# Both output products of a macaron block as seven quarter products for eight, on one Trainium2 core

## The chip, the cores and the metric

The kernel runs on one core of one Trainium2 chip. The metric is device time in microseconds (us), the median of several executions.

## The reference, cut to what matters

The block is two SwiGLU layers around an attention mixer, on x of 1024 tokens by D = 1024, all in float32. FF is 2816, 22 blocks of 128.

```python
def rms_norm(x, g):
    x32 = x.astype(jnp.float32)
    y = x32 * lax.rsqrt(jnp.mean(x32 * x32, axis=-1, keepdims=True) + EPS) * g.astype(jnp.float32)
    return y.astype(x.dtype)

def swiglu(h, w_in, w_out):
    gate, up = jnp.split(h @ w_in, 2, axis=-1)
    return (jax.nn.silu(gate) * up) @ w_out
...
    x = x + mix @ w_mix_out
    x = x + 0.5 * swiglu(rms_norm(x, ffn2_norm), ffn2_w_in, ffn2_w_out)
```

Before the mixer stands the first layer, `x + 0.5 * swiglu(rms_norm(x, ffn1_norm), ffn1_w_in, ffn1_w_out)`. The mixer projects the normed x, runs banded and compressed/selected attention, and projects back; nothing in it is touched but how its first projection begins.

## The kernel before, in words

**Precision.** A float32 product is made of three matmuls on operands that are split into a high and a low part (`mm3`, L248: high by high L249, high by low L250, low by high L251). Splitting a 128x512 tile is a copy to the high part on ScalarE (ACT) or GpSimd (POOL) and a subtraction for the low part on VectorE (DVE): `split` L445 with ACT L453 and DVE L457, or `conv` with POOL L87 and DVE L92.

**Order.** Nothing is ordered by hand. The program adds tasks, each with an engine, a cost, a position, what it depends on and the buffers it takes (`Slots`), to a `Plan` (L121). `Plan.run` picks, engine by engine, the task that can start first (the lowest position among those within 0.08) and emits it, so it sets the order of each engine's in-order queue. There are three plans: the first SwiGLU, the projection of the mixer, and attention with the second SwiGLU. All DMAs are issued from SyncE (SP), also in order.

**Input stage** (`first_stage` L566). h @ w_in is made block by block of FF. Two blocks are plain, twenty are seven products for eight (Strassen-Winograd): the operand of tokens is h in four quarters A11 to A22 and sums S1 to S4 of them, kept split in memory; the weights are quarters B11 to B22, which are the gate and up columns for the two halves of D, with differences T1 to T4 of them, made by `less` (L691, POOL, four a block) from raw tiles `wraw`. Each of the seven products of a block is 12 matmuls of 128x512. From banks P, R and Q come gate and up of the two token halves: `keep` L746 (ACT) copies a bank, `plus` L750 (DVE) adds another to it, silu L762 (ACT), and `times` L754 (POOL) multiplies silu(gate) by up. `put` stores the two results, 128x512 each, to DRAM tiles `gs`.

**Output stage** (`second_stage`). Eleven chunks of two FF blocks. For each block `gs` is loaded as a whole (`graw`, 128x1024, 512 KB), split by ACT L814 and DVE L816, and the two halves of w_out's 128 rows are loaded (`wraw`) and split by `conv`. Then each of 8 token tiles by 2 halves of D gets 6 matmuls in a bank of its own, and DVE adds half of the bank to the residual X (L846, `x<-lg,x`, 176 times). X was reloaded at the stage's start (`load_x`, or from XS in the second layer), since the input stage uses X's place for buffers.

**After the first output stage.** `norm_tile` (L531) norms a finished tile (`nxs`, DVE L537) and flips it by 8 transposes on TensorE (PE, `flip4`, L311) into a bank "a"; `flip_hi` and `flip_lo` make the split operand `xn`. Tiles 0 to 5 are in the first plan, 6 and 7 in the second, whose projection then runs with `xn` as the moving operand. The chunk's eight weight units are `CH3`, four of them split in the first plan.

Banks of PSUM: three "a", three "lg", one "pv", one "mo".

Of the kernel before, what the change touches and what calls it, by code (L numbers as in the profile page):

```python
# [8 lines left out]
F32 = mybir.dt.float32  # L9
# [9 lines left out]
T = 1024  # L19
# [168 lines left out]
def block_kernel(  # L188
# [118 lines left out]
    def flip4(src):  # L307

        p = bank("a", name="ntr")
# [126 lines left out]
    def fetch(src, pos, deps=()):  # L436
# [3 lines left out]
        def emit():  # L440
            b["r"] = ws.place()
            dma(b["r"].rearrange("p (k f) -> p k f", k=4), src)
# [3 lines left out]
    def split(b, dep, src_users, pos, eng):  # L446

        w, us = {}, []

        def high():  # L450
            w["h"], w["l"] = ws.pair()
# [4 lines left out]
        highs.append(add(eng, 0.6 if eng == "A" else 0.66, pos, high, deps=[dep], after=highs[-1:], takes=[(r_spl, us)]))  # L456
        low = add("D", 0.69, pos + 0.5, lambda: DVE.tensor_tensor(w["l"], b["r"], w["h"].bitcast(F32), op=OP.subtract),  # L457
                  deps=highs[-1:])
        src_users.extend([highs[-1], low])
# [60 lines left out]
    def flip_task(src, dst, t, pos, deps, free=()):  # L520

        b, au = {}, []
        p = add("P", 0.45, pos, lambda: b.update(p=flip4(src())), deps=deps, takes=[(r_a, au)])
# [5 lines left out]
    def norm_tile(t, pos, dep):  # L529
# [10 lines left out]
        for a in range(2):  # L540
            p, lo = flip_task(lambda a=a: xb["xs"][:, 512 * a:512 * a + 512], lambda a=a: blocks(xn[t // 4])[a], t, pos, [g])
# [24 lines left out]
    def first_stage(layer, w_in, opn, scaled, units_, pos, weigh, at0, pieces, opened, xa=()):  # L566
# [20 lines left out]
        stored_g = [[None, None] for _ in range(NF)]  # L587
# [11 lines left out]
        def put(n, half, buf, at, dep, us):  # L599
            t = add("S", 0.75, at, lambda: dma(GS[layer][n][:, HALF[half]], buf()), deps=[dep], tail=2.2)  # L600
            stored_g[n][half] = t
            us.append(t)

# [8 lines left out]
        for half in range(2):  # L612
            for n in range(PLAIN):
# [33 lines left out]
                put(n, half, lambda buf=buf: buf["u"], at, d, bu)  # L647
# [31 lines left out]
        av = Views([X[4][:, h] for h in HALF], [S3u(0), S1u(0)])  # L679
        dv = Views([X[5][:, h] for h in HALF], [S3u(1), S1u(1)])  # L680
        bv = Views([X[6][:, HALF[0]]], [S3u(2)])
        sv = Views([X[6][:, HALF[1]]], [S1u(2)])

        def less(a, b, at, deps):
# [1253 lines left out]
```

## Time and profile before

| what | us |
|---|---|
| median of three runs | 2025.47 (2023.34 to 2026.98) |
| the profiled execution | 2022.6 |
| its span | 2020.8 |
| PE busy in it | 1957.5 (97%) |
| DVE, ACT, POOL busy | 1249.0 (62%), 782.3 (39%), 692.2 (34%) |

The profile is one execution, with times in us from its start. A row of a timeline gives an instruction's start, its duration, engine, line and operation, and in brackets how long the engine was idle before it and what ended that. Matmuls overlap, so their spacing and not their duration is what one costs. A window's row gives the busy time of each engine in that stretch with the number of instructions, then the granted clock of PE as a share of the full one.

### The profile page before, as it was taken

How to read it: one execution, taken by the hardware profiler on the slowest of the kernel's cores; microseconds unless marked ns; L12 is line 12 of the kernel's file. 1: busy time of each engine (PE TensorE's matmuls, PEld its weight loads, DVE VectorE, ACT ScalarE, POOL GpSimd, SP SyncE). 2: the span in 40 equal slices, each digit the busy share in tenths (PEclk: the TensorE clock that was granted, in tenths of full speed). 3: DMA queues.
4: the chain of work that ended last, by engine and by line, in shares of the span. 5: the costliest groups of instructions: out<-in, count | busy, mean ns of one | idle time of the engine just before them, and what ended most of it. 6: DMA issues, size and time to landing. Idle time of an engine off the chain costs nothing.

```text
span 2020.8 us, 27799 instructions
## 1 busy us (share of the span) xinstructions
PE 1957.5 (97%) x9412; PEld 1632.3 (81%) x9412; DVE 1249.0 (62%) x2899; ACT 782.3 (39%) x1683; POOL 692.2 (34%) x792
## 2 busy tenths in 40 slices
PE   7999999998999989999899999989999999999999
PEld 6888888887888878887688778778888888878887
DVE  6554343335777776756888888875443333367765
ACT  4333333331001133344877888843333333311000
POOL 2254444441111111102754665533454344311110
PEclk9999999999999989999999999999999999999999
DMA  5132232236533116324201221012222222263322
GB/s 156 48 105 70 87 93 70 90 93 217 172 103 105 57 52 170 113 100 155 84 22 54 90 79 53 27 58 63 89 89 79 83 89 78 95 213 94 111 83 83
DMA packets 182461, 190.57 MB, mean 94 GB/s; under 512 B 18080, under 2 KB 132400, under 8 KB 182320
## 3 DMA queue, kind: packets, MB, share of 16 engines
q1 hardware_dynamic: 182320, 188.81, 29.9%
q8 instruction: 74, 1.21, 0.3%
q14 instruction: 67, 0.55, 0.1%
HBM read 142.47 MB, written 49.44 MB: 95 GB/s over the span
## 4 chain that ended last, share of the span: by engine, by line
PE 90%; DVE 3%; ACT 2%; POOL 2%; DMA 1%; issue 1%; SPq 0%; DVEq 0%; POOLq 0%; ACTq 0%
PE lg L249 15%; PE lg L250 15%; PE lg L251 15%; PE mo L249 6%; PE mo L251 6%; PE mo L250 6%; PE pv L249 5%; PE pv L250 5%; PE pv L251 5%; PE ptr L1740 3%; PE pvo L1760 2%; PE lg L1565 2%; PE pvo L1759 2%; PE ntr L311 2%; PE lg L1566 2%
## 5 line engine op out<-in xcount | busy, mean ns | idle before, releaser
L87 POOL TENSOR_SCALAR whi<-wraw 128x512 fp32r<-128x512 f32 (+1 forms) x140 | 95.9, 691 | 574.1 <-DVE x L846 281.6
L457 DVE TENSOR_TENSOR wlo<-wraw,whi 128x512 fp32r<-128x512 f32 x136 | 129.5, 957 | 158.9 <-ACT whi L453 147.8
L846 DVE SCALAR_TENSOR_TENSOR x<-lg,x 128x512 f32<-128x512 f32 x211 | 145.2, 688 | 82.9 <-PE lg L251 80.5
L814 ACT ACTIVATE gs<-graw 128x1024 fp32r<-128x1024 f32 x44 | 44.7, 1054 | 361.4 <-PE lg L251 237.0
L249 PE MATMUL lg<-whi,gs 128*128 128x512 f32 (+1 forms) x422 | 164.8, 391 | 0.0
L251 PE MATMUL lg<-whi,gs 128*128 128x512 f32 (+1 forms) x422 | 164.5, 390 | 0.0
L250 PE MATMUL lg<-wlo,gs 128*128 128x512 f32 (+1 forms) x422 | 164.4, 390 | 0.0
L457 DVE TENSOR_TENSOR wlo<-x,whi 128x512 fp32r<-128x512 f32 x104 | 82.0, 788 | 104.6 <-ACT whi L453 104.5
L754 POOL TENSOR_TENSOR x<-x,x 128x512 f32<-128x512 f32 x80 | 131.9, 1649 | 7.7 <-DVE x L750 6.6
L1750 DVE TENSOR_TENSOR pl<-ptr,ph 128x512 fp32r<-128x512 f32 x178 | 116.5, 685 | 16.2 <-ACT ph L1748 15.1
L746 ACT ACTIVATE x<-lg 128x512 f32<-128x512 f32 x96 | 57.3, 597 | 172.9 <-PE lg L251 172.9
L92 DVE TENSOR_TENSOR wlo<-wraw,whi 128x512 fp32r<-128x512 f32 (+1 forms) x140 | 100.9, 729 | 19.5 <-POOL whi L87 19.4
L1748 ACT ACTIVATE ph<-ptr 128x512 fp32r<-128x512 f32 x178 | 98.7, 595 | 33.2 <-PE ptr L1740 32.0
L453 ACT ACTIVATE whi<-wraw 128x512 fp32r<-128x512 f32 x120 | 75.1, 626 | 73.8 <-PE lg L250 43.0
L691 POOL TENSOR_TENSOR x<-wraw,x 128x512 f32<-128x512 f32 x38 | 51.8, 1364 | 148.5 <-DMA wraw<-in_ffn_w_in_dram 148.5
L691 POOL TENSOR_TENSOR x<-wraw 128x512 f32<-128x512 f32 x52 | 69.3, 1333 | 92.6 <-DMA wraw<-in_ffn_w_in_dram 92.6
L249 PE MATMUL lg<-xn0h,whi 128*128 128x512 f32 (+1 forms) x256 | 98.2, 383 | 0.0
L250 PE MATMUL lg<-xn0l,whi 128*128 128x512 f32 (+1 forms) x256 | 97.6, 381 | 0.2 <-DVE xn0l L319 0.2
L251 PE MATMUL lg<-xn0h,wlo 128*128 128x512 f32 (+1 forms) x256 | 97.5, 381 | 0.0
L750 DVE TENSOR_TENSOR x<-lg,x 128x512 f32<-128x512 f32 x72 | 49.8, 691 | 70.2 <-PE lg L251 70.2
L453 ACT ACTIVATE whi<-x 128x512 fp32r<-128x512 f32 x104 | 64.9, 628 | 73.1 <-PE lg L250 39.1
L249 PEld LDWEIGHTS lg<-whi,gs 128*128 128x128 f32 x422 | 79.8, 189 | 16.4
(464 smaller groups left out, 5746.8 us busy)
## 6 DMA issues: line engine op xcount, KB each, us to landing
wraw<-in_ffn_w_in_dram SPq DMA_DIRECT2D x176, 256.0 KB, 3.3
wraw<-in_ffn_w_out_dram SPq DMA_DIRECT2D x88, 256.0 KB, 2.7
graw<-gs SPq DMA_DIRECT2D x44, 512.0 KB, 3.5
gs<-x SPq DMA_DIRECT2D x80, 256.0 KB, 2.5
qd<-qst SPq DMA_DIRECT2D x32, 256.0 KB, 2.1
xn0l<-qd SPq DMA_DIRECT2D x32, 256.0 KB, 2.8
wraw<-in_w_mix_in_dram SPq DMA_DIRECT2D x28, 256.0 KB, 2.8
x<-in_x_dram SPq DMA_DIRECT2D x12, 512.0 KB, 7.0
```

What stands on the lines that cost most here:

```text
L87: self.nc.gpsimd.tensor_scalar(h[:, :width], self.raw[n][:, :width], 1.0, 1.0, op0=OP.mult, op1=OP.mult)
L92: self.nc.vector.tensor_tensor(l[:, :width], self.raw.pop(n)[:, :width], h[:, :width].bitcast(F32), op=OP.subtract)
L249: PE.matmul(o, ah, bh, start=first, stop=False, **kw)
L250: PE.matmul(o, ah, bl, start=False, stop=False, **kw)
L251: PE.matmul(o, al, bh, start=False, stop=last, **kw)
L453: ACT.activation(w["h"], b["r"], AF.Copy)
L457: low = add("D", 0.69, pos + 0.5, lambda: DVE.tensor_tensor(w["l"], b["r"], w["h"].bitcast(F32), op=OP.subtract), deps=highs[-1:])
L691: POOL.tensor_tensor(box["r"], a["r"], b["r"], op=OP.subtract)
L754: return add("G", 1.25, at, lambda a=tb[a], b=tb[b]: POOL.tensor_tensor(a["r"], a["r"], b["r"], op=OP.mult), deps=deps)
L846: x_ = add("D", 0.69, at, lambda box=box, t=t, d=d: DVE.scalar_tensor_tensor(X[t][:, d], box["o"], 0.5, X[t][:, d], op0=OP.mult, op1=OP.ad ...
L1748: ACT.activation(st["ph"], st["p"], AF.Copy)
L1750: lo = add("D", 0.6, pos + 0.2, lambda st=st: DVE.tensor_tensor(st["pl"], st["p"], st["ph"].bitcast(F32), op=OP.subtract), deps=[hi])
```

## The change

The output stage becomes seven products for eight as well. The quarters of its token operand are blocks of silu(gate) * up: A11 and A12 are the first token half of the even and the odd FF block of a pair, A21 and A22 the second half; there are eleven pairs k. The weights' quarters are the two blocks' rows of w_out by the two halves of D.

- The input stage stores the A quarters apart (`as`, 128x512), and after every odd block makes S1 to S4 of the pair on DVE, in place in the four buffers, and stores them too. The buffers' number goes from two to four for each of the two kinds.
- It also makes T1 to T4 of w_out's quarters in eleven side jobs of four loads, four subtractions on DVE and four stores (`sums_of`, DRAM tiles `ts`), spread over the twenty blocks; a twelfth job makes the S of the two plain blocks.
- `less` moves from POOL to DVE.
- The output stage runs product by product; each goes over all eleven k, and each k is 12 matmuls into four banks, of P ("a", "a", "a", "mo") or of R and Q ("lg", "lg", "lg", "pv"). Each k loads 256 KB of `as` (`graw`, split into `gph` and `gpl`) and 256 KB of w_out or `ts`, both split by ACT and DVE; POOL is not used. After a product four evictions add half of the banks to X. The last product's last three k are done tile by tile.
- The reload of X waits for every user of X's places. Tiles 0 to 3 are normed within the last product and flipped into "lg", tiles 4 to 7 in the projection's plan; all eight `CH3` units are split in the first plan. In the second layer the last stores are 512 columns wide (before, the last two were 256).

```diff
-    GS = [[dr.tile([128, T], F32, name=f"gs{k}_{n}") for n in range(NF)] for k in range(2)]
+    NK = NF // 2
+    AS = [[{a: dr.tile([128, 512], F32, name=f"as{k}_{n}{a}") for a in ("A11", "A12", "A21", "A22", "S1", "S2", "S3", "S4")}
+           for n in range(NK)] for k in range(2)]
+    TS = [[{a: dr.tile([128, 512], F32, name=f"ts{k}_{n}{a}") for a in ("T1", "T2", "T3", "T4")}
+           for n in range(NK)] for k in range(2)]
...
+        side_at = [Slots(1, u) for u in (S4u(2), S4u(3), list(scaled.values()), list(scaled.values()))]
+        side_in = lambda: [X[2][:, HALF[1]], X[3][:, HALF[1]], *side()]
+
+        def sums_of(k, at, srcs, deps, names, where, ops):
+
+            us, ld = [[] for _ in range(4)], []
+            for j in range(4):
+                ld.append(add("S", 0.75, at, lambda j=j: dma(side_in()[j], srcs[j]()), deps=deps, takes=[(side_at[j], us[j])],
+                              tail=2.2))
+            prev = ld
+            for name, (j, a, b, op) in zip(names, ops):
+                t = add("D", 0.69, at + 4.0, lambda j=j, a=a, b=b, op=op: DVE.tensor_tensor(
+                    side_in()[j], side_in()[a], side_in()[b], op=op), deps=prev)
...
+                put(k, name, lambda j=j: side_in()[j], at + 6.0, t, us[j], where)
+                prev = [t]
+            return us
...
         def less(a, b, at, deps):
...
-                POOL.tensor_tensor(box["r"], a["r"], b["r"], op=OP.subtract)
-            return box, add("G", 1.25, at, emit, deps=deps, after=[opened], takes=[(tv.slots, us)]), us
+                DVE.tensor_tensor(box["r"], a["r"], b["r"], op=OP.subtract)
+            return box, add("D", 0.69, at, emit, deps=deps, after=[opened], takes=[(tv.slots, us)]), us
...
+        jobs = [lambda at, k=k: sums_of(k, at, weights_of(k), [], *T_OPS) for k in range(NK)]
...
+        every = (NF - PLAIN) / (len(jobs) + 0.5)
         for n in range(PLAIN, NF):
+            while jobs and n - PLAIN >= every * (NK + 1 - len(jobs)):
+                side_us = jobs.pop(0)(at)
...
+            if j:
...
+                s1 = sum_(b22, b21, b22, ADD, [g21, g22, p22])
+                s3 = sum_(b21, b11, b21, SUB, [s1, g11])
+                s2 = sum_(b11, b22, b11, SUB, [s3, p11])
+                s4 = sum_(b12, b12, b11, SUB, [s2, g12, p12])
...
+                    put(k, name, lambda b=b: b["r"], at + 4.0, t, u)
...
+    PRODUCTS = (("A11", "B11", "P", 0, 0), ("A12", "B21", "R", 0, 0), ("S2", "T2", "P", 0, 1), ("S1", "T1", "Q", 1, 1),
+                ("S3", "T3", "P", 1, 1), ("S4", "B22", "Q", 0, 1), ("A22", "T4", "P", 1, 0))
+
+    def second_stage(layer, w_out, at, opened, first_free, stored, p_out, X_ready, each, last=3):
+
+
+        r_g, r_gp = Slots(5), Slots(8)
...
+        step = 12 * MM
+        pair = lambda: tuple(ring(p_out(), n, [128, 512], F32R, 8) for n in ("gph", "gpl"))
...
+        for m, (an, bn, bk, i, c) in enumerate(PRODUCTS):
...
+            tags = ("a", "a", "a", "mo") if bk == "P" else ("lg", "lg", "lg", "pv")
...
+            for k in range(NK):
+                p0 = at + k * step
...
+                loads_g.append(add("S", 0.75, p0 - 9.0, load, deps=[stored[k, an]] + first_, after=[opened, loads_g[-1]],
+                                   takes=[(r_g, ru)], tail=2.2))
+                A = split(b, loads_g[-1], ru, p0 - 5.0, "A", pair, r_gp, g_chain)
...
+                b, t, us = fetch(src, p0 - 9.0, dep, 1)
+                ops.append((A, split(b, t, us, p0 - 5.0, "A")))
...
+                mm3(O[tp], g["h"][:, col], g["l"][:, col], w["h"], w["l"], new and k == 0, k == NK - 1, skip_group_check=True)
...
+            for tp in range(4):
+                t = 4 * i + tp
+                x_ = add("D", 0.69, at, lambda t=t, c=c, tp=tp, O=O: DVE.scalar_tensor_tensor(
+                    X[t][:, HALF[c]], O[tp], 0.5, X[t][:, HALF[c]], op0=OP.mult, op1=OP.add), deps=[ends[tp]] + X_ready[t])
...
-    again = {t: [add("S", 1.46, at - 4.0 + t, lambda t=t: load_x(t), deps=gone[t], after=[opened], tail=2.2)]
+    again = {t: [add("S", 1.46, at - 4.0 + t, lambda t=t: load_x(t), deps=gone, after=[opened], tail=2.2)]
              for t in range(NT)}
...
-        if d.stop == D and t < NT - 2:
-            norm_tile(t, pos + 1.0, pend[t])
+    def each(t, c, x_, pos):
+        if c == 1 and t < 4:
+            norm_tile(t, pos + 1.0, [x_], "lg")
...
-    norm_tile(6, at, [none])
-    norm_tile(7, at + 4.0, [none])
+    for t in range(4, NT):
+        norm_tile(t, at + 2.0 * (t - 4), [none])
```

Three places of the order show what moves. First TensorE's queue at the end of the first output stage. Before (ntr is a flip's bank, nxs a normed tile, xn0h and xn0l the split operand of the projection):

```order
L251 MATMUL mo_5628<-whi_5277,gs_5281 128x512
L311 MATMUL ntr_5637<-ident_82,nxs_5569 128x128 x4
L311 MATMUL ntr_5643<-ident_82,nxs_5569 128x128 x4
L311 MATMUL ntr_5661<-ident_82,nxs_5616 128x128 x4
L311 MATMUL ntr_5666<-ident_82,nxs_5616 128x128 x4
L311 MATMUL ntr_5685<-ident_82,nxs_5656 128x128 x4
L311 MATMUL ntr_5690<-ident_82,nxs_5656 128x128 x4
L249 MATMUL lg_5752<-whi_5290,xn0h_89 128x512
L250 MATMUL lg_5752<-wlo_5291,xn0h_89 128x512
```

After, where 24 matmuls into mo_6269 follow the last product and precede these rows, all but the last left out here:

```order
L251 MATMUL mo_6269<-whi_6210,xn0l_90 128x512
L249 MATMUL lg_6322<-whi_5993,xn0h_89 128x512
L250 MATMUL lg_6322<-wlo_5994,xn0h_89 128x512
L251 MATMUL lg_6322<-whi_5993,xn0l_90 128x512
L311 MATMUL ntr_6332<-ident_82,nxs_6267 128x128 x4
L311 MATMUL ntr_6337<-ident_82,nxs_6267 128x128 x4
L249 MATMUL lg_6322<-whi_6052,xn0h_89 128x512
L250 MATMUL lg_6322<-wlo_6053,xn0h_89 128x512
L251 MATMUL lg_6322<-whi_6052,xn0l_90 128x512
L311 MATMUL ntr_6350<-ident_82,nxs_6280 128x128 x4
```

The flips of three tiles that stood together between the two stages are now among the projection's matmuls, and the projection starts in the bank mo.

Second, VectorE's queue in the first input stage. Before, some eleven blocks in (x4 to x6 are the buffers of `keep`, `plus` and `times`, ext and x0 to x3 hold T):

```order
L750 TENSOR_TENSOR x5_79<-pv_1332,x5_79 128x512
L457 TENSOR_TENSOR wlo_1446<-ext1_180,whi_1445 128x512
L750 TENSOR_TENSOR x6_80<-lg_1395,x6_80 128x512
L457 TENSOR_TENSOR wlo_1464<-wraw_1329,whi_1463 128x512
L457 TENSOR_TENSOR wlo_1487<-wraw_1371,whi_1486 128x512
L457 TENSOR_TENSOR wlo_1508<-x1_75,whi_1507 128x512
L750 TENSOR_TENSOR x4_78<-lg_1493,x4_78 128x512
```

After, at the turn from an odd block to the next (L729 is `less`, L839 an S sum, L795 `plus`, L459 the low part of a split):

```order
L729 TENSOR_TENSOR x3_77<-wraw_2579,x1_75 128x512
L459 TENSOR_TENSOR wlo_2713<-wraw_2579,whi_2712 128x512
L459 TENSOR_TENSOR wlo_2735<-x1_75,whi_2734 128x512
L839 TENSOR_TENSOR x5_79<-x5_79 128x512
L795 TENSOR_TENSOR x7_81<-lg_2718,x7_81 128x512
L839 TENSOR_TENSOR x5_79<-x4_78,x5_79 128x512
L459 TENSOR_TENSOR wlo_2754<-x0_74,whi_2753 128x512
L839 TENSOR_TENSOR x4_78<-x5_79,x4_78 128x512
L729 TENSOR_TENSOR ext0_399<-wraw_2737,wraw_2710 128x512
L839 TENSOR_TENSOR x4_78<-x4_78 128x512
L459 TENSOR_TENSOR wlo_2778<-x2_76,whi_2777 128x512
```

Between the splits and additions stand now `less` and the S sums, the first of which waits for a store; the addition of the next block's first product stands right behind it.

Third, SyncE's queue where the first output stage begins. Before:

```order
L256 DMA gainm_3699<-in_mix_norm_dram 128x1024
L256 DMA gqa_3701<-in_q_norm_a_dram 128x64
L256 DMA gka_3702<-in_k_norm_a_dram 128x64
L256 DMA gqb_3705<-in_q_norm_b_dram 128x64
L256 DMA gkb_3706<-in_k_norm_b_dram 128x64
L256 DMA graw_3715<-gs0_0_110 128x1024
L256 DMA graw_3721<-gs0_1_111 128x1024
L256 DMA gs0_21_131<-x4_78 128x512
L256 DMA x0_74<-in_x_dram 128x1024
L256 DMA x1_75<-in_x_dram 128x1024
```

After, behind the same gainm and small gains:

```order
L256 DMA gkb_4132<-in_k_norm_b_dram 128x64
L256 DMA graw_4141<-as0_0A11_110 128x512
L256 DMA graw_4143<-as0_1A11_118 128x512
L256 DMA as0_10A12_191<-x7_81 128x512
L256 DMA graw_4151<-as0_2A11_126 128x512
L256 DMA graw_4154<-as0_3A11_134 128x512
L256 DMA as0_10A22_193<-x1_75 128x512
L256 DMA graw_4164<-as0_4A11_142 128x512
```

The first load of the stage keeps its place and is half as large, and the reloads of X no longer follow it directly.

## Rows read from the trace of the kernel before

**Rows 1.** The page: busy time by engine, and the chain's shares.

```profile
PE 1957.5 (97%) x9412; PEld 1632.3 (81%) x9412; DVE 1249.0 (62%) x2899; ACT 782.3 (39%) x1683; POOL 692.2 (34%) x792
...
PE 90%; DVE 3%; ACT 2%; POOL 2%; DMA 1%; issue 1%; SPq 0%; DVEq 0%; POOLq 0%; ACTq 0%
```

**Rows 2.** PE's timeline, first output stage: start us, us, operation.

```profile
689.79 0.39 PE L250 MATMUL lg<-wlo,gs 128*128 128x512 f32 x1
...
695.68 0.39 PE L249 MATMUL lg<-whi,gs 128*128 128x512 f32 x1
```

**Rows 3.** Waits of PE over the span: us in total, times, longest.

```profile
PE mo L249 <- ACT gs L814: 7.9, 2, 5.7
```

**Rows 4.** PE's timeline, first input stage to first output stage.

```profile
467.43 0.39 PE L251 MATMUL lg<-A22h,wlo 128*128 128x512 f32 x1
473.53 0.77 PE L249 MATMUL mo<-whi,gs 128*128 128x512 f32 x1 [5.71 <-ACT gs L814]
```

**Rows 5.** Windows: us, busy (x count) by engine, PEclk, DMA share, GB/s.

```profile
100.00:200.00 100.00, 100.00 (x443) 82.83 (x442) 50.71 (x58) 38.02 (x66) 48.70 (x35) 1.00 0.29 88
473.50:483.50 10.00, 9.97 (x36) 7.57 (x37) 5.83 (x7) 1.06 (x1) 0.00 (x0) 0.84 1.03 413
493.50:560.00 66.50, 66.50 (x295) 55.10 (x294) 50.22 (x103) 6.04 (x6) 8.21 (x12) 1.00 0.54 162
1775.00:1785.00 10.00, 9.14 (x31) 6.83 (x32) 5.23 (x6) 1.06 (x1) 0.15 (x1) 0.83 1.03 376
```

**Rows 6.** PE's timeline, from the first output stage to the projection.

```profile
717.71 1.12 PE L311 MATMUL ntr<-ident,nxs 128*128 128x128 f32 x8
721.63 1.33 PE L311 MATMUL ntr<-ident,nxs 128*128 128x128 f32 x8 [2.81 <-DVE nxs L537]
726.91 1.95 PE L311 MATMUL ntr<-ident,nxs 128*128 128x128 f32 x8 [3.95 <-DVE nxs L537]
728.52 0.78 PE L249 MATMUL lg<-whi,xn0h 128*128 128x512 f32 x1
...
732.51 0.53 PE L249 MATMUL lg<-whi,xn0h 128*128 128x512 f32 x1
...
740.15 1.60 PE L311 MATMUL ntr<-ident,nxs 128*128 128x128 f32 x12
741.51 0.48 PE L249 MATMUL lg<-whi,xn0h 128*128 128x512 f32 x1
```

**Rows 7.** The page, costliest groups: evictions and ACT's copies.

```profile
L846 DVE SCALAR_TENSOR_TENSOR x<-lg,x 128x512 f32<-128x512 f32 x211 | 145.2, 688 | 82.9 <-PE lg L251 80.5
L814 ACT ACTIVATE gs<-graw 128x1024 fp32r<-128x1024 f32 x44 | 44.7, 1054 | 361.4 <-PE lg L251 237.0
...
L453 ACT ACTIVATE whi<-wraw 128x512 fp32r<-128x512 f32 x120 | 75.1, 626 | 73.8 <-PE lg L250 43.0
```

**Rows 8.** Groups by line and shape, 100 to 460 us, DVE, POOL.

```profile
L457 DVE TENSOR_TENSOR wlo<-wraw,whi 128x512 fp32r<-128x512 f32 x55 | 57.1, 1039 | 73.5 <-ACT whi L453 73.5
...
L457 DVE TENSOR_TENSOR wlo<-ext,whi 128x512 fp32r<-128x512 f32 x26 | 19.3, 744 | 22.9 <-ACT whi L453 22.9
...
L754 POOL TENSOR_TENSOR x<-x,x 128x512 f32<-128x512 f32 x38 | 61.2, 1611 | 3.2 <-DVE x L750 2.9 <-ACT x L746 0.3
L691 POOL TENSOR_TENSOR x<-wraw 128x512 f32<-128x512 f32 x24 | 31.7, 1321 | 43.8 <-DMA wraw<-in_ffn_w_in_dram 43.8
```

**Rows 9.** The page, DMA issues: KB each, median us to landing.

```profile
wraw<-in_ffn_w_out_dram SPq DMA_DIRECT2D x88, 256.0 KB, 2.7
graw<-gs SPq DMA_DIRECT2D x44, 512.0 KB, 3.5
gs<-x SPq DMA_DIRECT2D x80, 256.0 KB, 2.5
```

**Rows 10.** SyncE's timeline, first loads of the first output stage.

```profile
466.55 0.91 SPq L256 DMA_DIRECT2D graw<-gs  x2
```

**Rows 11.** Waits of SyncE's queue, 100 to 460: us, times, longest.

```profile
SPq L256 <- DVE wlo L457: 204.1, 35, 8.0
```

More of the change, by code (lines that the diff above doesn't have):

```diff
@@ L441, in emit, with split @@
             b["r"] = ws.place()
-            dma(b["r"].rearrange("p (k f) -> p k f", k=4), src)
+            dma(b["r"].rearrange("p (k f) -> p k f", k=k) if k > 1 else b["r"], src)
         fetched.append(add("S", 0.75, pos, emit, deps=deps, after=fetched[-1:], takes=[(r_raw, us)], tail=2.2))
         return b, fetched[-1], us
-    def split(b, dep, src_users, pos, eng):
+    def split(b, dep, src_users, pos, eng, pair=ws.pair, slots=None, chain=None):
         w, us = {}, []
+        chain = highs if chain is None else chain
         def high():
-            w["h"], w["l"] = ws.pair()
+            w["h"], w["l"] = pair()
             if eng == "A":
@@ L455, in high @@
                 POOL.tensor_scalar(w["h"], b["r"], 1.0, 1.0, op0=OP.mult, op1=OP.mult)
-        highs.append(add(eng, 0.6 if eng == "A" else 0.66, pos, high, deps=[dep], after=highs[-1:], takes=[(r_spl, us)]))
+        chain.append(add(eng, 0.6 if eng == "A" else 0.66, pos, high, deps=[dep], after=chain[-1:],
+                         takes=[(slots or r_spl, us)]))
         low = add("D", 0.69, pos + 0.5, lambda: DVE.tensor_tensor(w["l"], b["r"], w["h"].bitcast(F32), op=OP.subtract),
-                  deps=highs[-1:])
-        src_users.extend([highs[-1], low])
+                  deps=chain[-1:])
+        src_users.extend([chain[-1], low])
         return w, low, us
@@ L564, in open_in, with first_stage @@
         return t
-    def first_stage(layer, w_in, opn, scaled, units_, pos, weigh, at0, pieces, opened, xa=()):
+    def first_stage(layer, w_in, w_out, opn, scaled, units_, side, pos, weigh, at0, pieces, opened, xa=()):
         ready = {}
@@ L597, in product, with put @@
                     last and a == 3, skip_group_check=True)
-        def put(n, half, buf, at, dep, us):
-            t = add("S", 0.75, at, lambda: dma(GS[layer][n][:, HALF[half]], buf()), deps=[dep], tail=2.2)
-            stored_g[n][half] = t
+        def put(k, name, buf, at, dep, us, where=AS):
+            t = add("S", 0.75, at, lambda: dma(where[layer][k][name], buf()), deps=[dep], tail=2.2)
+            stored[k, name] = t
             us.append(t)
+            return t
         W = {}
@@ new lines, in first_stage, with sum_ @@
+            if j:
+                (g11, b11, u11, p11), (g12, b12, u12, p12), (g21, b21, u21, _), (g22, b22, u22, p22) = (
+                    half_done[i] for i in range(4))
+                def sum_(o, a, b, op, deps, at=at):
+                    return add("D", 0.69, at + 2.0, lambda: DVE.tensor_tensor(o["r"], a["r"], b["r"], op=op), deps=deps)
+                s1 = sum_(b22, b21, b22, ADD, [g21, g22, p22])
+                s3 = sum_(b21, b11, b21, SUB, [s1, g11])
+                s2 = sum_(b11, b22, b11, SUB, [s3, p11])
+                s4 = sum_(b12, b12, b11, SUB, [s2, g12, p12])
+                for name, t, b, u, more in (("S1", s1, b22, u22, [s1, s2]), ("S3", s3, b21, u21, [s1, s3]),
+                                            ("S2", s2, b11, u11, [s3, s2, s4]), ("S4", s4, b12, u12, [s4])):
+                    u.extend(more)
+                    put(k, name, lambda b=b: b["r"], at + 4.0, t, u)
```

186 lines of the change are left out of this document (97 added, 89 removed).

## The prediction, made before the changed kernel was run

> **What bounds the kernel now.** I read the busy times and the chain of waits first [rows 1]. TensorE (PE) is busy 97% of the span and holds 90% of the chain, VectorE (DVE) 3%, ScalarE (ACT) 2%, DMA 1%. So the time is the number of matmuls by their spacing, plus the few places where PE stands or runs at a low clock. The profiled execution took 2022.6 us with a span of 2020.8; it lies 2.9 under the median of 2025.5, and I add these 2.9 at the end.
>
> The spacing comes from PE's timeline in the output stage of the first SwiGLU [rows 2]: 27 matmuls with 26 steps between 689.79 and 695.68, 0.2266 us each. The 0.39 us in a row is a matmul's pipelined duration, not its price. Twelve of them (one 128-row block of FF against four token tiles) are 2.72 us.
>
> The places where PE stands show in its waits and in its timeline. Before each output stage it waits for the first split of `gs`: 7.9 us in two times, the longer 5.7 [rows 3]. The input stage ends with the matmul of 467.43 and the output stage starts at 473.53 [rows 4], and the windows [rows 5] show that it starts at a granted clock of 0.84, 36 matmuls in 10 us where 44 fit (10 / 0.2266). The second start is as slow: 31 matmuls at 0.83. After the first output stage PE does nothing from 717.71 to 728.52 but three pairs of flips, with 2.81 and 3.95 us of idle time before them, and the first nine matmuls of the projection take from 728.52 to 732.51, 0.44 us each: the lower level of its clock, 1.2 GHz, where 0.2266 is the upper, 2.4 [rows 6].
>
> **Output stages.** Before, a stage is 22 blocks x 8 token tiles x 2 halves of D x 3 matmuls = 1056. Seven products for eight quarter products make 7 x 11 x 4 x 3 = 924. That is 132 fewer, 132 x 0.2266 = 29.9 us a stage, **-59.8** for both, if PE is fed. Per 2.72 us step it now needs one 256 KB load of A and one of w_out, two ACT copies and two DVE subtractions.
> - ACT: 2 x 0.626 = 1.25 us [rows 7].
> - DVE: 2 x 0.744 to 2 x 1.039 = 1.5 to 2.1 us [rows 8], and 28 evictions of 0.688 us [rows 7] a stage where there were 176. The old stage held DVE 50.2 of 66.5 us, and PE was busy all 66.5 [rows 5].
> - DMA: 512 KB in 2.72 us is 193 GB/s. The window 493.5 to 560 moved 162 at a share of 0.54, so 193 would be a share of about 0.64; the window at 473.5 moved 413 [rows 5].
>
> So the loads, ACT and DVE lie beside PE, at nothing. Their cover is the 2.72 us of matmuls; without it an eighth of a microsecond in each of 154 steps would cost 19 us. Between two products on one set of banks lies one on the other, 30 us, so evictions are hidden too.
>
> The Trainium skill (DMA: Bandwidth & Descriptors, Anatomy of one DMA) speaks against smaller transfers: some 2.0 us fixed for each plus the bytes at 436 GB/s, an estimate of 2.6 us for 256 KB. The rows agree on a single one, 2.7 us for w_out and 3.5 us for the 512 KB of `gs` [rows 9]. Paid one after another, two in each step would take 5.2 us where PE takes 2.72. The 413 GB/s show that they run side by side.
>
> **Starts of the output stages.** SP issues the first two loads of `graw` at 466.55, behind gainm and four small gains, in 0.91 us [rows 10]; in the new order the same five issues stand ahead. The first load is half as large and only ACT's high part of 0.626 us stands before PE. With 2.7 to 3.5 us of landing PE starts at 469.9 to 470.7; with the transfer as slow as it was (the matmul at 473.53 had a copy of 1.05 before it [rows 7]), at 473.53 - 1.05 + 0.63, about 473. I take 471.2, nearer to the landing times: **-2.3** (0 to -3.6). The slow clock behind it I leave as it is. In FFN2 the wait is 2.2 us [rows 3] and the ten microseconds behind it lose 13 matmuls, 2.9 us [rows 5]; the shorter load and copy give **-1.0** (0 to -2).
>
> All eight X tiles are now reloaded after the first thirteen `graw`, 4.2 MB, 10 us at 413 GB/s, and the loads of operands queue behind them on SP. The ring of split operands is eight steps deep, 8 x 2.72 = 21.8 us, so it should hold: **+1** for both stages (0 to +6).
>
> **From output to projection.** All 64 flips remain: four tiles inside the last product (three before), four between the matmuls of the projection. A warm flip is 1.36 us / 12 = 0.113 (740.15 to 741.51 [rows 6]), so the 24 flips between 717.71 and 728.52 are worth 2.7 us of 10.8, and 8.1 are lost. The nine slow matmuls lose 3.99 - 2.04 = 1.95 more. Of these 10.05 us the new order gives back all but one wait: the first projection matmul takes bank mo, the last product's own, and waits for its eviction, about 0.3 + 0.69. What is late next are the flips of t4, 27 matmuls or 6.1 us in; with nothing between them, a pair waited at most 3.95 us for its normed tile [rows 6], so 6.1 us of matmuls ahead of the first should cover it. Net **-9.0** (-10 to -3, if the flips come late and the clock falls again).
>
> **Input stages.** PE's products are the same. POOL loses four subtractions a block, about 1.32 us each [rows 8], DVE gets them, and 4 sums for each of 11 pairs of output weights, of 11 pairs of A: (80 + 88) / 20 = 8.4 instructions a block more. Nearest rows: 0.744 us (`wlo<-ext`) and 1.039 (`wlo<-wraw`, beside a busy POOL), so 6.2 to 8.7 us. DVE was busy 50.71 of 100 us, 9.7 of a block of 7 x 2.72 = 19.04 us [rows 5]; now 15.9 to 18.4 of 19.04. It fits, and POOL with two products a block disturbs it less. A block that holds a job of each kind (12 new ones) needs up to 22 us, 3 over; operands are split several products ahead, which covers that. SP gets 8 DMAs for a job of T and 4 for one of S, some 135 a stage; at 0.91 / 2 us of issue each [rows 10] that is 61 of 381 us, in a queue that mostly waits [rows 11]. I take **+1.5** a stage (0 to +7), **+3**.
>
> **End.** The last eviction is 512 wide instead of 256, 0 to +0.69: **+0.3**.
>
> Sum: -59.8 - 2.3 - 1.0 + 1.0 - 9.0 + 3.0 + 0.3 = -67.8. 2022.6 - 67.8 = 1954.8, and 2.9 more on the median's scale: **1957.7**.
>
> **Rivals.**
> 1. *Small stalls in the input stage.* DVE's in-order queue now holds instructions that wait for DMAs: the first S sum of a pair overwrites A22 and waits until its store has landed, and behind it stand the additions and splits that PE wants. 1.2 us for each of 22 pairs is 26 us: 1957.7 - 3 + 26 = 1981. For it: DVE at 84 to 97% of a block. Against: PE was busy 100 of 100 us in the old stage, with DVE idle half of them [rows 5].
> 2. *Slower: the store of A22 is late.* Same place, other mechanism. After the product's end E come silu 0.63, POOL's product 1.61 [rows 8] and the landing 2.5 [rows 9], so the sum runs at about E + 5. The addition queued behind it must be through before the fourth product of the next block at E + 8.16, which leaves some 2 us. SP waits in order for freed buffers, 204.1 us in 35 times, up to 8.0 [rows 11]. A store behind such a wait is 8 us late, PE stands 6 us in each of 22 pairs, 132 us: 2087. It decides from 68 / 22 = 3.1 us a pair, a store some 5 us late. Against: the plan sets the loads that SP waits with 14 us ahead of their use, and the store behind the buffer's release.
> 3. *Transfers bind the output stage.* By rows, one after another, 2 x 2.7 us a step: 154 x (5.4 - 2.72) = 413 us more, 2371. The page named above gives that by its fixed cost (2.6 us each, about the same). The 413 GB/s [rows 5] speak against it.
> 4. *The turns give nothing*: the flips come late, the gaps stay. -59.8 + 3.3 + 1: 1970.
>
> **How the numbers follow.** The forecast 0.71, rival 1 0.17, rival 2 0.04, rival 3 0.02, rival 4 0.06. The low end takes the best bounds, -59.8 - 3.6 - 2 - 10 = -75.4: 1950, and 3 us for what I overlooked: 1947. The high end reaches just past rival 1: 1985. A measurement here tells about 0.2%, 4 us, from no change. Faster 0.93 (forecast, rivals 4 and 1, less 0.01 for worse stalls), same 0.01, slower 0.06.
>
> **What would show it.** Right: 264 matmuls fewer, PE 97% or more, each output stage about 209 us plus flips; no PE wait over 1 us within the stages; first output matmul near 471; no run of lone flips after the stage. Wrong: PE waits on DVE's additions or splits in the input stage, repeating every two blocks (rivals 1, 2); a step of over 2.72 us with ACT waiting for `graw` (rival 3); a wait for `nxs` of several microseconds and a fallen clock at the projection (rival 4).

## The result, and the profile after

The changed kernel takes 1959.5 us (median of four runs, 1957.4 to 1961.0) where the kernel before takes 2025.3 in the same comparison: a ratio of 0.9675, 95% interval 0.9661 to 0.9688. The forecast was 1957.7, range 1947 to 1985. The profiled execution, the fastest of the four, took 1957.4 us, span 1955.7.

The page of the changed kernel, its busy times and its chain [rows 1]:

```profile
PE 1895.3 (97%) x9142; PEld 1580.6 (81%) x9142; DVE 1358.0 (69%) x3114; ACT 917.2 (47%) x1947; POOL 405.2 (21%) x544
...
PE 82%; DVE 7%; DMA 5%; ACT 2%; issue 2%; SPq 1%; POOL 1%; DVEq 0%; ACTq 0%; POOLq 0%
```

TensorE has 270 instructions fewer, the 264 forecast and six more because the last results are no longer made in halves of 256 columns, and is as full as before, 97%. Its share of the chain fell from 90 to 82%, VectorE's rose from 3 to 7 and DMA's from 1 to 5: the stretches in which PE stands are ended by other engines than before. PE's waits over the span say where [rows 3]:

```profile
PE a L249 <- ACT gph L454: 5.7, 2, 4.4
...
PE pv L249 <- DVE x L795: 3.6, 2, 2.5
...
PE lg L249 <- DVE x L795: 1.4, 1, 1.4
...
PE mo L249 <- DVE x L795: 1.2, 1, 1.2
...
PE mo L249 <- DVE x L922: 0.9, 1, 0.9
```

L454 is the copy of a split, L795 the addition `plus` of the input stage, L922 the eviction. The waits on L795 (3.6, 1.4 and 1.2 us) are new. PE's timeline at the two turns of the first layer [rows 4, 6], the last of each stage and the first of the next:

```profile
472.21 0.39 PE L251 MATMUL lg<-A22h,wlo 128*128 128x512 f32 x1
477.01 0.80 PE L249 MATMUL a<-whi,gph 128*128 128x512 f32 x1 [4.40 <-ACT gph L454]
477.60 0.63 PE L250 MATMUL a<-wlo,gph 128*128 128x512 f32 x1
```

```profile
692.96 0.39 PE L251 MATMUL mo<-whi,gpl 128*128 128x512 f32 x1
694.22 0.47 PE L249 MATMUL mo<-whi,xn0h 128*128 128x512 f32 x1 [0.88 <-DVE x L922]
```

The first output matmul still waits 4.4 us and the matmuls behind it run 0.43 us apart, at the lower level of the clock (1.2 GHz). The projection follows the output stage after 1.26 us, and its matmuls run 0.23 us apart, at the upper level (2.4 GHz). The windows [rows 5], for the two halves of the first input stage and for both output stages:

```profile
100.00:280.00 180.00, 176.28 (x770) 145.13 (x769) 137.50 (x198) 66.02 (x114) 27.10 (x18) 0.99 0.71 231
280.00:460.00 180.00, 180.00 (x796) 149.05 (x795) 115.75 (x151) 66.09 (x114) 28.85 (x20) 1.00 0.34 108
500.00:690.00 190.00, 190.00 (x854) 157.95 (x853) 119.30 (x232) 87.17 (x152) 4.13 (x6) 1.00 0.67 214
1760.00:1950.00 190.00, 190.00 (x840) 157.39 (x839) 97.42 (x154) 73.94 (x127) 0.00 (x0) 1.00 0.65 209
```

The output stages move 209 to 214 GB/s and PE is busy all through. In the first half of the input stage PE misses 3.7 us, with 231 GB/s moved; the second half, with 108 GB/s, misses none.

From timelines like these, stretch by stretch (from the start of a stretch's first matmul to that of the next one's; us):

| stretch | before | after | difference |
|---|---|---|---|
| to the first matmul with S2 | 91.5 | 91.1 | -0.4 |
| first input stage, to its last matmul | 376.0 | 381.1 | +5.1 |
| gap to the first output matmul | 6.1 | 4.8 | -1.3 |
| first output stage, to its last matmul | 244.0 | 216.0 | -28.0 |
| gap to the projection | 11.0 | 1.3 | -9.8 |
| projection and attention, to the mixer's output product | 241.9 | 240.7 | -1.2 |
| that product and attention, to its last matmul | 369.2 | 369.3 | +0.1 |
| second input stage, to its last matmul | 432.8 | 435.2 | +2.4 |
| gap to the second output stage | 2.6 | 1.7 | -0.9 |
| second output stage, to its last matmul | 242.3 | 210.3 | -32.0 |
| to the end of the span | 3.5 | 4.3 | +0.8 |

The sum is -65.2, the spans differ by 65.1.

### The profile page after: what moved, and what is told of

It reads as the page before. It is cut to its first block, busy times and chain, and to the rows that moved or that the text cites. A ratio compares the mean times of both kernels' runs of the same rounds, so it can differ in the third digit from the quotient of the medians.

```text
span 1955.7 us, 28018 instructions
## 1 busy us (share of the span) xinstructions
PE 1895.3 (97%) x9142; PEld 1580.6 (81%) x9142; DVE 1358.0 (69%) x3114; ACT 917.2 (47%) x1947; POOL 405.2 (21%) x544
## 4 chain that ended last, share of the span: by engine, by line
PE 82%; DVE 7%; DMA 5%; ACT 2%; issue 2%; SPq 1%; POOL 1%; DVEq 0%; ACTq 0%; POOLq 0%
PE lg L249 11%; PE lg L251 11%; PE lg L250 11%; PE mo L249 5%; PE mo L251 5%; PE mo L250 5%; PE pv L249 3%; PE pv L251 3%; PE pv L250 3%; PE ptr L1815 3%; PE a L251 3%; PE a L249 3%; PE a L250 3%; PE pvo L1835 2%; PE lg L1640 2%
## 5 line engine op out<-in xcount | busy, mean ns | idle before, releaser
L459 DVE TENSOR_TENSOR wlo<-wraw,whi 128x512 fp32r<-128x512 f32 x290 | 220.1, 764 | 88.3 <-ACT whi L454 76.7
L799 POOL TENSOR_TENSOR x<-x,x 128x512 f32<-128x512 f32 x80 | 117.7, 1473 | 717.0 <-DVE x L795 675.7
L454 ACT ACTIVATE whi<-wraw 128x512 fp32r<-128x512 f32 x274 | 170.7, 623 | 126.8 <-PE lg L250 41.5
L459 DVE TENSOR_TENSOR gpl<-graw,gph 128x512 fp32r<-128x512 f32 x154 | 106.9, 697 | 131.5 <-ACT gph L454 131.1
L454 ACT ACTIVATE gph<-graw 128x512 fp32r<-128x512 f32 x154 | 96.8, 631 | 174.9 <-PE pv L250 82.0
L249 PE MATMUL a<-whi,gph 128*128 128x512 f32 x264 | 104.2, 395 | 5.7 <-ACT gph L454 5.7
L251 PE MATMUL a<-whi,gpl 128*128 128x512 f32 x264 | 103.6, 392 | 0.7 <-DVE gpl L459 0.7
L250 PE MATMUL a<-wlo,gph 128*128 128x512 f32 x264 | 103.5, 392 | 0.0
L454 ACT ACTIVATE whi<-x 128x512 fp32r<-128x512 f32 x104 | 64.9, 628 | 73.2 <-PE lg L250 35.9
L459 DVE TENSOR_TENSOR wlo<-x,whi 128x512 fp32r<-128x512 f32 x104 | 71.4, 686 | 22.8 <-ACT whi L454 22.8
L795 DVE TENSOR_TENSOR x<-lg,x 128x512 f32<-128x512 f32 x72 | 49.6, 689 | 45.2 <-PE lg L251 45.1
L249 PE MATMUL lg<-whi,gph 128*128 128x512 f32 x198 | 77.0, 389 | 0.0
L250 PE MATMUL lg<-wlo,gph 128*128 128x512 f32 x198 | 77.0, 389 | 0.0
L251 PE MATMUL lg<-whi,gpl 128*128 128x512 f32 x198 | 77.0, 389 | 0.0
```

The source lines that it names most:

```text
L249: PE.matmul(o, ah, bh, start=first, stop=False, **kw)
L250: PE.matmul(o, ah, bl, start=False, stop=False, **kw)
L251: PE.matmul(o, al, bh, start=False, stop=last, **kw)
L795: return add("D", 0.69, at, lambda b=tb[k], o=bx[o]: DVE.tensor_tensor(b["r"], o["o"], b["r"], op=OP.add), deps=deps)
L799: return add("G", 1.25, at, lambda a=tb[a], b=tb[b]: POOL.tensor_tensor(a["r"], a["r"], b["r"], op=OP.mult), deps=deps)
```

## The experiments

The main steps hold, but the input stages lost 7.5 us where 3 were forecast. The queue of VectorE (DVE) before the longest of the new stops, and PE's row there:

```profile
155.91 0.69 DVE L729 TENSOR_TENSOR x<-wraw 128x512 f32<-128x512 f32 x1 [4.21 <-DMA wraw<-in_ffn_w_in_dram]
157.29 0.69 DVE L706 TENSOR_TENSOR x<-x,x 128x512 f32<-128x512 f32 x1 [0.69 <-DMA x<-in_ffn_w_out_dram]
...
159.95 0.69 DVE L706 TENSOR_TENSOR gain<-gain 128x512 f32<-128x512 f32 x1
...
161.16 0.68 DVE L795 TENSOR_TENSOR x<-pv,x 128x512 f32<-128x512 f32 x1
```

```profile
161.90 0.79 PE L249 MATMUL pv<-A22h,whi 128*128 128x512 f32 x1 [2.50 <-DVE x L795]
...
163.35 0.63 PE L249 MATMUL pv<-A22h,whi 128*128 128x512 f32 x1
```

The engine stands 4.21 us at a weight difference (L729) whose raw weights have not landed, then works through the sums of a side job (L706), and the addition that PE's bank waits for comes at 161.16, 2.5 us late. The seven matmuls behind it run at the lower level of the clock, some 0.43 us apart. The other three stops look alike: at 197.92, 1424.63 and 1465.19 a difference (L729) starts after 4.91, 2.92 and 3.30 us of idle time for its raw weights, and the job's four sums stand between it and the late addition. SyncE's queue ahead of the first stop:

```profile
149.13 0.38 SPq L256 DMA_DIRECT2D gain<-in_ffn_w_out_dram  x1
149.56 1.22 SPq L256 DMA_DIRECT2D wraw<-in_ffn_w_in_dram  x2
150.87 1.45 SPq L256 DMA_DIRECT2D x<-in_ffn_w_out_dram  x2
```

The two raw tiles (`wraw`) go out between two pairs of a job's loads and land 5.5 and 5.7 us after their issue; in the kernel before, a raw tile took 3.3 us on the median. At the other stops the order is the same, and they took 4.1 to 5.0 us. Four readings fit: the differences on DVE's queue (A), the job's loads, a DVE that is simply full (B), or rival 2, the S sum that waits for a store.

**`less` back on GpSimd (POOL).**

```diff
-                DVE.tensor_tensor(box["r"], a["r"], b["r"], op=OP.subtract)
-            return box, add("D", 0.69, at, emit, ...
+                POOL.tensor_tensor(box["r"], a["r"], b["r"], op=OP.subtract)
+            return box, add("G", 1.25, at, emit, ...
```

> The changed kernel with the weight differences T1 to T4 of the input stage (`less`) back on GpSimd. Theory A (VectorE's in-order queue: a difference that waits for its raw weights holds up the additions behind it): the four waits of TensorE for x L795 (2.5, 1.2, 1.4, 1.1 us) vanish, and with them the stretch at the low clock after the longest; the first input stage ends 4 to 6 us earlier (466 to 468 instead of 472.4), the second is 2 to 3 us shorter, span 1947 to 1950. Rival B (VectorE is simply full, or the sums of w_out's quarters hold the queue on their own loads): removing four of some 18 instructions a block is not enough, waits of 1 us and more on L795 remain, span within 2 us of 1955.7.

Span 1966.8, above the ranges of both readings; the input stages take 385.1 and 440.3 us, longer than with `less` on DVE (381.1 and 435.2). PE's waits in the first one:

```profile
PE lg L249 <- DVE x L795: 5.4, 3, 2.5
```

Theory A in this form falls: the stops stay when the differences leave DVE's queue. That they cost more on POOL is only suggested here, since four executions with the same input stages (the changed kernel and three runs below that edit other stages) spread from 379.0 to 383.2 and from 435.2 to 438.3 us; the run with the jobs spread and `less` on POOL shows it.

**The side jobs without their loads.**

```diff
-            for j in range(4):
+            for j in range(4 if k == 0 else 0):
...
```

> The changed kernel without the loads of w_out's quarters in the side jobs of the input stages, except for the first job and the one for the plain blocks: the four sums and four stores of each job stay, but work on what lies in the buffers. It leaves out 40 loads of 256 KB a stage, so T1 to T4 are not w_out's. Theory A with its cause in the burst of four loads (it lets the raw weights of the input stage land late): the differences find their weights there, VectorE's idle time before L729 falls from 1 to 4 us to under 1, the waits on L795 vanish, span 1948 to 1951. Rival B (VectorE full): the same number of VectorE instructions, the waits stay, span 1954 to 1957.

Span 1949.6, input stages of 375.3 and 432.1 us, as short as before the change, with the same number of DVE instructions and no wait on L795. DVE's waits for raw weights in the first input stage (92 to 466 us), in the changed kernel and then in this one, where `less` is L730:

```profile
DVE x L729 <- DMA wraw<-in_ffn_w_in_dram: 14.8, 7, 4.9
```

```profile
DVE x L730 <- DMA wraw<-in_ffn_w_in_dram: 2.5, 3, 1.5
```

14.8 us in 7 times (18.1 with the differences that go into `ext`) became 2.5 in 3. So the loads of the jobs are what stops PE, and DVE is not full: the same sums stand in its queue and stop nothing. The loads also hold the queue directly, since the sums wait for them, 9.1 us in this stage of the changed kernel and 0.3 here, but between the difference and the addition of a stop that is 0.7 and 0.9 us in two of the four and nothing in the others.

**The gains later.**

```diff
-        load_gain(mem["gain"], mix_norm)
...
+    small = add("S", 2.0, at_out + 12.0, small_gains, deps=again[NT - 1], after=[opened], tail=2.2)
```

> The changed kernel with the loads of gainm and of the four small gains moved on SyncE from ahead of the first output stage's loads to behind the reload of X. Theory: the five issues ahead (2.4 us) and gainm's 512 KB beside the first load are what makes the first output matmul wait; it starts 0.5 to 2 us after the input stage instead of 4.6, and as in the second layer (1.4 us of gap, matmuls 0.23 us apart) the clock does not fall, so another 2.5 us of slow matmuls go: span 1949 to 1952. Rival: the first load is late for its own sake (it waits for the store or for the place that it takes) and starts at the same time: gap over 4 us, span 1955.

```profile
470.85 0.39 PE L251 MATMUL lg<-A22h,wlo 128*128 128x512 f32 x1
472.50 0.50 PE L249 MATMUL a<-whi,gph 128*128 128x512 f32 x1 [1.26 <-ACT gph L454]
...
473.89 0.50 PE L251 MATMUL a<-whi,gpl 128*128 128x512 f32 x1 [0.66 <-DVE gpl L459]
```

The gap is 1.65 us where it was 4.8, and the clock stays at its upper level: the first output stage takes 214.3 us against 216.0. That is 3.1 us of the gap, as expected, and 1.7 of the slow matmuls, where 2.5 were expected: 4.8 in all. The span fell by only 1.3, to 1954.4, and missed the expected 1949 to 1952. In this execution the first input stage was 2.1 us shorter and the second 2.8 longer (379.0 and 438.1 us), the second output stage 1.6 longer, the first matmul with S2 came 0.7 later and the projection took 0.7 more.

**Tiles 4 and 5 flipped first.**

```diff
-        if c == 1 and t < 4:
+        if (c == 1 and t < 4) or (c == 0 and t in (4, 5)):
...
```

> The changed kernel with tiles 4 and 5 normed and flipped at the end of the first plan, as before the change, instead of among the projection's matmuls; only 6 and 7 stay there. Theory: the turn from the output stage to the projection is where some 9 us of the gain come from; the flips of t4 and t5 stand alone again on TensorE, wait 6 to 9 us for evictions and normed tiles, and the projection starts at the low clock: span 1962 to 1966. Rival: the turn is short because the last product's evictions are few and early, whatever the order: the gap grows by under 3 us, span under 1959.

```profile
698.26 1.20 PE L311 MATMUL ntr<-ident,nxs 128*128 128x128 f32 x8 [1.79 <-DVE nxs L540]
703.23 1.95 PE L311 MATMUL ntr<-ident,nxs 128*128 128x128 f32 x8 [3.77 <-DVE nxs L540]
704.84 0.78 PE L249 MATMUL mo<-whi,xn0h 128*128 128x512 f32 x1
```

The lone flips are back with waits of 1.79 and 3.77 us, the gap is 8.8 us (1.3), and the projection starts at the lower level. From the last output matmul to the mixer's output product it is 249.2 us against 242.0: the place of these two tiles is worth 7.2 us. The span, 1970.1, lies above the 1962 to 1966 expected: the input stages took 383.2 and 437.8 us, 4.7 more together than in the changed kernel, the first matmul with S2 came 1.5 later and the mixer's second stretch took 1.6 more.

**The side jobs spread.** The jobs were placed over the twenty blocks, but a position only breaks ties in the plan; they ran as soon as their places came free, which is why the first half moved 231 GB/s. One dependency holds each back:

```diff
-                ld.append(add("S", 0.75, at, lambda j=j: dma(side_in()[j], srcs[j]()), deps=deps,
+                ld.append(add("S", 0.75, at, lambda j=j: dma(side_in()[j], srcs[j]()), deps=[*deps, chain[-1]],
```

> The changed kernel with one dependency more in the plan: the loads of a side job (w_out's quarters) start after the last matmul of the block ahead of which the job is placed, so the twelve jobs lie over all twenty blocks. In the changed kernel they run as soon as their places are free, and the first half of the input stage moves 231 GB/s and the second 108 (100 to 280 and 280 to 460 us). Theory A2 (it is the bunched loads: raw weights land late, VectorE's queue stops at the differences, additions behind it come late): both halves move 160 to 180 GB/s, VectorE's waits for raw weights fall from 18 us to under 6, at most one wait of TensorE on L795 is left and it is under 1 us; both input stages are as long as in the kernel before (376 and 433 us from S2 to the end, now 381 and 435): span 1947 to 1950. Rival C (a job disturbs its own block wherever it lies, by its four sums in the queue and by its loads): the waits move to other blocks and their sum stays at 5 to 8 us: span 1953 to 1957.

```profile
100.00:280.00 180.00, 180.00 (x796) 149.05 (x795) 134.29 (x180) 67.89 (x117) 29.24 (x20) 1.00 0.52 166
280.00:460.00 180.00, 180.00 (x796) 149.05 (x795) 125.33 (x171) 67.00 (x116) 26.04 (x18) 1.00 0.54 177
```

166 and 177 GB/s, and PE misses nothing in either half; there is no wait on L795 in either layer. The input stages take 375.3 and 432.1 us, the span is 1949.6; DVE waits 6.5 us for raw weights in the first one, a little over the 6 expected. A2 holds: the loads are as many as in the changed kernel, and only their time is another. Single raw tiles still took up to 7.0 us to land, so slow landings alone don't stop PE; how much of the lateness was landing time and how much a later issue was not separated. The span fell by 6.1 us, less than the 8.9 of the input stages, because the mixer's second stretch took 1.7 more and the second output stage 1.6.

**No S sums.**

```diff
-                    return add("D", 0.69, at + 2.0, lambda: DVE.tensor_tensor(o["r"], a["r"], b["r"], op=op), deps=deps)
+                    return add(None, 0.0, at + 2.0, lambda: None, deps=deps)
```

> The changed kernel without the four sums S1 to S4 after every odd block of the input stages (40 VectorE instructions a stage): the four stores remain and store the quarters as they are, so S1 to S4 are left out of the output stage's operands. It takes away the wait for the store of A22 that rival 2 of the prediction is about. By the theory A2 the stops come from the side jobs' loads: waits of TensorE on L795 remain at 3 to 8 us in sum, input stages stay 2 to 6 us longer than before, span 1951 to 1955. By rival 2 (the S sum waits for the store and holds the addition behind it) they vanish: span 1946 to 1949.

Span 1953.1, input stages of 377.9 and 435.9 us. The waits on L795 stay, 2.1 us in the first layer and 1.9 in the second, and the first half still moves 232 GB/s:

```profile
100.00:280.00 180.00, 177.93 (x784) 146.79 (x783) 133.13 (x186) 66.96 (x116) 29.06 (x20) 1.00 0.71 232
```

So rival 2 is not what cost most of the time in the changed kernel. A share of about 1 us in the first layer can't be excluded, since 377.9 lies under the 379.0 to 383.2 of the executions with the sums.

**Every load of A twice.**

```diff
                     dma(b["r"], AS[layer][k][an])
+                    dma(ring(p_out(), "spare", [128, 512], F32, 4), AS[layer][k][an])
```

> The changed kernel with every load of A in both output stages made twice, the second time into four spare buffers that nobody reads, and the ring of A's split pairs cut from eight to six to make room. A step of 2.72 us now moves 768 KB, 289 GB/s. It measures how far the output stage is from being bound by its transfers. If transfers run side by side and have room (forecast): the two output stages are 216 and 210 us long as before, within 3 us each; only the first microseconds, where X is reloaded, may stall: span 1955 to 1962. If the queue pays a fixed price for each transfer (rival 3): steps grow from 2.72 to some 4 us (three landings of 2.7 us over two), 100 us and more a stage: span over 2100.

```profile
500.00:690.00 190.00, 189.41 (x847) 156.48 (x846) 118.73 (x232) 87.15 (x154) 4.44 (x6) 1.00 0.89 311
1760.00:1940.00 180.00, 179.98 (x794) 148.62 (x794) 99.60 (x157) 76.53 (x133) 0.00 (x0) 1.00 0.94 333
```

The output stages take 216.5 and 212.2 us (216.0 and 210.3 in the changed kernel), moving 311 and 333 GB/s. The change's own 209 to 214 GB/s lie a third under a rate at which PE still hardly waits; rival 3 is out.

**Jobs spread and gains later.** Both edits above together.

> Both edits that looked right: the side jobs spread over the blocks (as in the run on that) and the gains behind the reload of X. If the two are independent: input stages as long as before the change (376 and 433 us), the first output matmul within 2 us of the input stage's end and no stretch at the low clock behind it: span 1942 to 1946, about 5 us under the run with the jobs spread alone. If the stops at the side jobs vary from run to run whatever their place: span 1947 to 1953.

Median 1949.8 us of five runs, ratio 0.9621 (0.9608 to 0.9634), clear of the changed kernel's interval. The input stages are 375.3 and 432.1, the gap 1.65 us. But the profiled span is 1948.7, not 1942 to 1946; one of the five executions (span 1942.7) was in that range, the others were not. In the profiled one the first output stage took 215.9 us, not 214.3, because the clock fell this time after the same two waits, and the second took 211.9, not 210.3:

```profile
469.54 0.50 PE L249 MATMUL a<-whi,gph 128*128 128x512 f32 x1 [1.27 <-ACT gph L454]
...
470.93 0.50 PE L251 MATMUL a<-whi,gpl 128*128 128x512 f32 x1 [0.66 <-DVE gpl L459]
...
472.53 0.63 PE L250 MATMUL a<-wlo,gph 128*128 128x512 f32 x1
```

Another 1.9 us lie in the mixer, whose second stretch took 371.2 us here and 369.3 in the changed kernel; no edit touches it, and why it differs stayed open.

**Jobs spread, `less` on POOL.**

> The side jobs spread over the blocks and `less` back on GpSimd. With the jobs bunched, `less` on GpSimd made the input stages longer (385 and 440 us from S2 to the end against 381 and 435) instead of shorter as theory A had it. Two causes are left for that. D: only the bunched loads stop TensorE, and slower subtractions on GpSimd (1.4 to 1.7 us) had merely less slack behind a late raw weight; spread, both engines do, and the input stages are 376 and 433 us, span 1948 to 1951 as with the jobs spread alone (1949.6). E: GpSimd's two-input instructions slow VectorE's beside them (a sum or a low part takes 1.0 instead of 0.7 us on the mean), and with 8 instructions more a block VectorE's queue then runs late by itself: waits of TensorE on L795 come back in the spread version too, 3 to 10 us in sum, span 1953 to 1960.

Span 1958.3, input stages of 379.7 and 435.6 us where the same jobs with `less` on DVE gave 375.3 and 432.1: reading D falls, and the waits of reading E are there (4.1 us in both layers, on L795 and the splits). So the differences do cost more on POOL. One of them, followed back over POOL, SP, DVE and PE:

```profile
394.93 1.30 POOL L729 TENSOR_TENSOR x<-wraw 128x512 f32<-128x512 f32 x1
396.18 1.29 POOL L799 TENSOR_TENSOR x<-x,x 128x512 f32<-128x512 f32 x1
```

```profile
397.50 0.33 SPq L256 DMA_DIRECT2D as_8A<-x  x1
```

```profile
403.45 0.69 DVE L839 TENSOR_TENSOR x<-x,x 128x512 f32<-128x512 f32 x1 [2.37 <-DMA as_8A<-x]
...
405.87 1.78 DVE L839 TENSOR_TENSOR x<-x,x 128x512 f32<-128x512 f32 x1
...
411.19 0.67 DVE L795 TENSOR_TENSOR x<-lg,x 128x512 f32<-128x512 f32 x1
```

```profile
411.92 0.50 PE L249 MATMUL lg<-A22h,whi 128*128 128x512 f32 x1 [0.69 <-DVE x L795]
```

The product of the A22 half (L799) stands on POOL's queue behind a `less`, its store is issued at 397.50 and lands 5.9 us later beside a job's loads, the S sum (L839) starts at 403.45 after DVE has idled 2.37 us for it, the third of the sums runs for 1.78 us beside POOL, and the addition of 411.19 makes PE wait 0.69. That is the mechanism of rival 2, at a small price, and it appears when POOL has `less` to do. DVE idles 12.2 us for such stores in the first input stage here, 2.4 with the jobs spread and `less` on DVE. How much of the loss is this wait and how much DVE's slower instructions was not separated.

**The tile in mo first.** On top of the jobs spread and the gains later.

```diff
-            for tp in range(4 if cut < NK else 0):
+            for tp in (3, 0, 1, 2) if cut < NK else ():
```

> The fastest version so far (jobs spread, gains behind the reload of X) with the last product's tile in bank mo made first of the four instead of last, so that its eviction is over when the projection's first matmul takes that bank. Theory: the wait of 0.9 us for x L922 at the projection goes and nothing else changes: the gap between the last output matmul and the projection falls from 1.26 to 0.23 us, 1 us less in all, which is under what the rounds can tell from the version without it (1949.8 us); median 1945 to 1950. Rival: the wait moves to the flips of tile 4 or to another bank, and the projection's later start shows it: the gap falls and the first matmul of the mixer's output product comes no earlier.

```profile
684.11 0.39 PE L251 MATMUL a<-whi,gpl 128*128 128x512 f32 x1
684.34 0.39 PE L249 MATMUL mo<-whi,xn0h 128*128 128x512 f32 x1
```

The gap is 0.23 us and nothing moved behind it: 240.7 us to the mixer's output product, 240.9 without the edit. The median of 1948.0 us (ratio 0.9622, 0.9609 to 0.9635) cannot be told from the run without it, as expected. It has the lowest median; both versions beat both kernels.

## Why the prediction was right, step by step

- **Output stages.** -59.8 was forecast and PE was fed: 924 matmuls at 0.2266 are 209.4 us, and the second stage took 210.3. The bounds on ACT, DVE and DMA held with room: DVE was busy 119.3 and ACT 87.2 of 190 us in the first stage's window, and the doubled loads showed it for DMA. The fixed cost that the prediction takes from the Trainium skill (DMA: Bandwidth & Descriptors, Anatomy of one DMA) is stated there for DMAs issued from GpSimd; all of this kernel's are issued from SyncE, and for those the rows carry the argument (2.7 us for 256 KB).
- **Starts.** First layer: -2.3 forecast, -1.3 measured. The first load landed only 5.0 us after its issue, beside gainm, where the forecast took 2.7 to 3.5; that the gains were in the way was in the text, not its price. The first output matmul came at 477.0 and not near 471, because the input stage ended 4.8 us later as well. Second layer: -0.9 in the gap against -1.0, and 2.1 us beyond the matmuls removed inside the stage, since the clock did not fall. The text left the slow clock as it was, and this gain is in part luck: in five of the experiments the clock fell there and the stage took 1.6 us more.
- **Reload of X.** +1 was forecast; no wait shows it.
- **From output to projection.** -9.0 was forecast; the gap and the projection give -11.0, with 0.9 of flips that moved into the output stage. The wait for bank mo was 0.88 us, the flips of tile 4 did not wait. The edit that puts back the flips of two tiles costs 7.2; the rest of the 11 was not tested by itself.
- **Input stages.** +3 was forecast and +7.5 measured. The step that was mis-sized is "operands are split several products ahead, which covers that": it weighed instructions, and the stops come from the additions, which are not ahead of anything, behind differences whose weights land late while four loads of a job are in flight. The forecast took the jobs as spread over twenty blocks by their position; they were not. Rival 1 named the place (DVE's queue behind a DMA) and put 26 us on it as regular stops for every pair; there were four of 1.1 to 2.5 us, so the sign "no PE wait over 1 us within the stages" failed in the input stages. The instructions were priced too high: with the jobs spread DVE was busy 72% of 100 to 460 us, 13.7 of a block's 19.04 us, where 15.9 to 18.4 were forecast. In other executions with the same input stages the stops cost 3 to 7 us in the first layer and 2 to 5 in the second.
- **End.** +0.3 forecast, +0.8 measured.

In sum the spans moved 2.7 us less than forecast (by the medians the forecast is 1.8 off). Worse than forecast were the input stages by 4.5, the first output stage by 1.9 (0.9 of it the flips), the first start by 1.0 and the end by 0.5; better were the second output stage by 2.1, the turn to the projection by 2.0, the reload by 1.0 and the start of the span by 0.4. The mechanisms were right in the main, but that the total is so near owes something to errors that cancel.

## What to carry to other kernels

When extra transfers are hung beside a stage that is bound elsewhere, look at when they will run, not only at how many: this kernel's scheduler, for which a position only breaks ties, ran them as early as it could, and then they delayed the loads that the stage needed. On an in-order queue, ask of each new instruction what it waits for and what stands behind it that has no slack; counting busy time answers neither. At the turn between two stages, the order in which independent work is queued counts too: 7.2 us here for two tiles, beside 60.0 in the output stages.

## What was not expected of the hardware

A DVE instruction on 128x512 with two operands in SBUF takes 0.69 us, and up to 1.78 us in these rows while POOL runs one of its own. In the changed kernel, DVE and then POOL:

```profile
184.72 0.68 DVE L459 TENSOR_TENSOR wlo<-wraw,whi 128x512 fp32r<-128x512 f32 x1
185.32 1.78 DVE L729 TENSOR_TENSOR ext<-wraw,ext 128x512 f32<-128x512 f32 x1
187.02 1.78 DVE L706 TENSOR_TENSOR gain<-gain,x 128x512 f32<-128x512 f32 x1
188.72 0.68 DVE L729 TENSOR_TENSOR x<-wraw 128x512 f32<-128x512 f32 x1
```

```profile
184.94 3.31 POOL L799 TENSOR_TENSOR x<-x,x 128x512 f32<-128x512 f32 x2 [16.46 <-DVE x L795]
```

It is not always so much: in the kernel before, 77 low parts (L457) that lie wholly beside POOL's instructions with two inputs took 1.12 us on the mean, 0.69 to 1.87, and the 164 that lie beside none 0.69. The additions of `plus`, which read one operand from PSUM, take 0.69 us on the mean at 128x512 in all kernels, also the 36 of the kernel before that lie wholly beside POOL's. The Trainium skill (GPSIMD Engine Reference, Key points) says that POOL shares its SBUF interfaces with VectorE and that VectorE's instructions with two SBUF inputs contend with it; these rows agree and give the price.

The same two waits at the start of an output stage, 1.27 and 0.66 us, were followed by the lower clock level in some executions and not in others: the second output stage took 210.3 us in the changed kernel and in four of the experiments, and 211.9 in five others. What decides it stayed open.
